# Side work of a hybrid attention and retention block issued in pairs between the dense matmuls

## The chip, the cores and the metric

One core of a Trainium2 chip. The time is the device time of one execution in microseconds; lower is better. The engines work in parallel and meet by semaphores: TensorE (PE; its weight loads are PEld), VectorE (DVE), ScalarE (ACT), GpSimd (POOL) and SyncE (SP), whose queue issues nearly all loads.

## The reference

One layer over 512 tokens of width 1024, in float32:

```python
h = rms_norm(x, norm_gain)
sb_q, sb_k, sb_v, sb_g, r_q, r_k, r_v, r_g, m_sb, m_ret = split(h @ w_in)
# attention, 8 heads of 128: w[t,s] = sigmoid(z) * prod over s<j<t of (1 - sigmoid(z_j)), s < t
out_a = stick_breaking(rms_norm(q), rms_norm(k), v) * silu(sb_g)
# retention, 4 heads of 256: (q.k) * gamma^|t-s| over the same chunk of 64 and all earlier ones
out_b = rms_norm(retention(rotary(r_q), rotary(r_k) / 16, r_v)) * silu(r_g)
merged = sigmoid(m_sb + b0) * (out_a @ w_branch_sb) + sigmoid(m_ret + b1) * (out_b @ w_branch_ret)
y = x + merged @ w_out
```

## The kernel before

Every float32 operand is split in a high and a low half (`split`: ScalarE copies the high half, VectorE subtracts for the low one), and each product is three matmuls (`mm3`): high x high, high x low, low x high.

**Dense groups.** `dense` makes one 512 x 512 output over 8 blocks of k and 4 banks j: 96 matmuls of 512 columns, twelve for each k. Their order: qk0, v0, sg0, qk1, qk2, v1, sg1, qk3, ma0, rqk0, pa0, ma1, pa1, rg0, then the value projection of the retention in products of quarters (rv), rqk1, rqk2, rg1, rqk3, mb0, mb1, pb0, pb1, fin0, fin1. PSUM has 5 banks for them and 3 (`side_psum`) for the side work.

**Side work.** Everything small on TensorE is written as generators, and `Interleaver` runs them between the dense matmuls: `dense` calls `work.step()` (L249) after every six of them (after j = 1 and j = 3, not after the last of the group), so a group has 15 steps. A generator that yields n is resumed n steps later. There is one queue, first in, first out (only `token_sums` is put at its head): the next generator starts when the one ahead of it has ended, in the same step. `matmul`, `transpose` and `load` are kept in program order (`tc.keep_in_program_order`), so the order of these calls is the order on TensorE and on SP; the other engines' order is planned by the framework.

**What the generators do.** `post` of `qk_group` waits 8 steps (W_QK) and transposes the normed q and k, four transposes for each of 4 blocks of tokens, with ScalarE and VectorE making their halves. `attention` works on two heads of 4 blocks each, 8 blocks; in round n it issues the scores of block n (L577 on: three matmuls, VectorE's mask, two sigmoids on ScalarE, a scan and a product on VectorE), the values of a head whose fourth block was weighted in the round before (twelve matmuls, the gate, a split), and the weights of block n - 2 (b + 1 transposes, a split into `wT_pair`), each followed by a yield of 1 (W_Z, W_W). Scores of block b are at least 256 and up to 512 columns wide. `retention` issues four score pieces (`rz`, 2 steps apart, W_RZ), two value pieces (`ro`) and two pieces of four transposes (`rt`).

**Where it must be done.** `work.drain(ready)` resumes the head of the queue until a condition holds, without regard to what it yields and without dense matmuls between. `pa0` multiplies the attention's outputs: its act for block k is `branch_act(oa)`, which drains until head k's output `oa[k]` is made. `ret(0)` (its dense group is rqk0) drains until `oa[5]` is there, rotates q and k on VectorE (`rope_group`) and adds the generator of retention head 0.

Of the kernel before, what the change touches and what calls it, by code (L numbers as in the profile page):

```python
# [15 lines left out]
NT = S // P  # L16
# [22 lines left out]
W_QK, W_Z, W_W = 8, 1, 1  # L39
W_RQ, W_RZ, W_RO, W_RN = 8, 2, 2, 5  # L40
# [32 lines left out]
def hybrid_block(ctx, tc, x, x_t, vecs, w_in, w_rv, w_a, w_b, w_o, cos_t, sin_t, decay, out):  # L73
# [13 lines left out]
    def f32(ap):  # L87
        return ap.bitcast(F32)
# [4 lines left out]
    def transpose(*a):  # L93
        tc.keep_in_program_order(nc.tensor.transpose(*a))

    def mm3(ps, a, b, first, last):

        matmul(ps, a[0], b[0], start=first, stop=False)
        matmul(ps, a[0], b[1], start=False, stop=False)
        matmul(ps, a[1], b[0], start=False, stop=last)  # L100

    def side_psum(name):
        return ps_a.tile([P, S], F32, tag="a", name=name)

    def T_tile(name, dtype=F32R):
        return big.tile([P, 4, S], dtype, tag="T", bufs=4, name=name)
# [14 lines left out]
    def bk_tile(name, dtype=F32):  # L121
        return tmp.tile([P, 2, S], dtype, tag="bk", bufs=3, name=name)
# [3 lines left out]
    def tmp_tile(name):  # L126
        return tmp.tile([P, S], F32, tag="tmp", name=name)
# [74 lines left out]
    def rsqrt(dst, ssq, n, width):  # L202
        t = small.tile([P, 16], F32, tag="ms", name="ms")
        nc.vector.tensor_scalar(t[:, :width], ssq, 1.0 / n, EPS, op0=ALU.mult, op1=ALU.add)  # L204
        nc.gpsimd.tensor_tensor(dst, t[:, :width], m_half[:, :width], op=ALU.pow)  # L205
# [49 lines left out]
    def proj(name, blocks, rows):  # L255
        return dense(name, lambda k: (xT_hi[:, k, :], xT_lo[:, k, :]), w_in, blocks, rows)
# [44 lines left out]
    def qk_group(p):  # L301

        ps = proj(f"qk{p}", ((C_Q + 256 * p, 256), (C_K + 256 * p, 256)), True)
        ss = small.tile([P, NT, 4], F32, tag="ss", name=f"ss{p}")
        raws = []
        for tb in range(NT):
            raw = tmp.tile([P, 4, P], F32, tag="qraw", bufs=4, name=f"qraw{p}_{tb}")
            nc.scalar.copy(raw, ps[tb].rearrange("p (h d) -> p h d", h=4))
            raws.append(raw)
        for tb in range(NT):  # L310
            sq = tmp_tile("sqq").rearrange("p (h d) -> p h d", h=4)
            nc.scalar.activation(sq, raws[tb], AF.Square)
            nc.vector.reduce_sum(ss[:, tb, :], sq, axis=mybir.AxisListType.X)
        rr = small.tile([P, NT, 4], F32, tag="rr", name=f"rr{p}")
        nc.vector.tensor_mul(ss, ss, rx2.rearrange("p (b o) -> p b o", o=1).broadcast_to([P, NT, 4]))
        rsqrt(rr.rearrange("p b h -> p (b h)"), ss.rearrange("p b h -> p (b h)"), HD, 16)
        nc.gpsimd.tensor_mul(rr, rr, rx.rearrange("p (b o) -> p b o", o=1).broadcast_to([P, NT, 4]))
        for tb in range(NT):
            nc.gpsimd.tensor_tensor(
                raws[tb], raws[tb],  # L320
                rr[:, tb, :].rearrange("p (h o) -> p h o", o=1).broadcast_to([P, 4, P]), op=ALU.mult,
            )

        def post():
            hi, lo = T_tile(f"qk_hi{p}"), T_tile(f"qk_lo{p}")
            yield W_QK
            for tb in range(NT):
                pt = side_psum(f"pqk{p}_{tb}").rearrange("p (h d) -> p h d", h=4)
                for j in range(4):
                    transpose(pt[:, j, :], raws[tb][:, j, :], ident)  # L330
                ts = slice(tb * P, (tb + 1) * P)
                for c, a in ((V_QG, 0), (V_KG, 2)):
                    g = vec[:, c : c + 1]
                    nc.scalar.activation(hi[:, a : a + 2, ts], pt[:, a : a + 2, :], AF.Copy, scale=g)
                    nc.vector.scalar_tensor_tensor(
                        lo[:, a : a + 2, ts], pt[:, a : a + 2, :], g, f32(hi[:, a : a + 2, ts]),
                        op0=ALU.mult, op1=ALU.subtract,
                    )
                yield 1
            qk_parts[p] = (hi, lo)  # L340

        work.add(post())
        if p == 0:
            work.add(token_norm_rows())
# [207 lines left out]
    def attention(heads, ready, v, gates):  # L552

        blocks = [(h, b) for h in heads for b in range(NT)]
        beta = {}

        def scores(h, b):
            hi, lo = qk_parts[h // 2]
            a, n = h % 2, (b + 1) * P
            ts = slice(b * P, n)  # L560
            z = side_psum(f"z{h}_{b}")
            m = max(n, 256)
            mm3(z[:, :m], (hi[:, a, ts], lo[:, a, ts]), (hi[:, 2 + a, :m], lo[:, 2 + a, :m]), True, True)
            nc.vector.tensor_add(z[:, ts], z[:, ts], neg_mask)  # L564
            bk = bk_tile(f"beta{h}_{b}")
            bt, keep = bk[:, 0, :], bk[:, 1, :]
            nc.scalar.activation(keep[:, :n], z[:, :n], AF.Sigmoid, scale=-sc)  # L567
            nc.scalar.activation(bt[:, :n], z[:, :n], AF.Sigmoid, scale=sc)
            nc.vector.tensor_tensor_scan(  # L569
                keep[:, :n][:, ::-1], keep[:, :n][:, ::-1], zero.broadcast_to([P, n]), 1.0,  # L570
                op0=ALU.mult, op1=ALU.add,
            )
            nc.vector.tensor_mul(bt[:, : n - 1], bt[:, : n - 1], keep[:, 1:n])
            beta[h, b] = bt

        def weights(h, b):
            hi, lo = wT_pair  # L577
            bt = beta.pop((h, b))
            pw = side_psum(f"pw{h}_{b}").rearrange("p (i t) -> p i t", t=P)
            for i in range(b + 1):  # L580
                transpose(pw[:, i, :], bt[:, i * P : (i + 1) * P], ident)
            ts = slice(b * P, (b + 1) * P)
            split(hi[:, : b + 1, ts], lo[:, : b + 1, ts], pw[:, : b + 1, :])

        def values(h):
            hi, lo = wT_pair
            po = side_psum(f"po{h}")
            cs = slice((h % 4) * P, (h % 4 + 1) * P)
            vv = v()
            for i in range(NT):  # L590
                t0 = min(i, NT - 2) * P
                mm3(po[:, t0:], (vv[i][0][:, cs], vv[i][1][:, cs]), (hi[:, i, t0:], lo[:, i, t0:]),
                    i == 0, i == NT - 1)
            o = tmp_tile(f"oa{h}")
            nc.vector.tensor_mul(o, po, gates()[h % 4])
            oa[h] = O_pair(f"oa{h}")
            split(oa[h][0], oa[h][1], o)

        for n in range(len(blocks) + 3):
            if n < len(blocks):  # L600
                scores(*blocks[n])
                yield W_Z
            if n >= 3 and blocks[n - 3][1] == NT - 1:
                while not ready():
                    yield 1
                values(blocks[n - 3][0])
                yield W_Z
            if 2 <= n < len(blocks) + 2:
                weights(*blocks[n - 2])
                yield W_W  # L610

    def rope_group(h, ready):

# [22 lines left out]
    def retention(h, qk, v, gates, made):  # L636
# [7 lines left out]
        for i in range(NT):  # L644
            n = S - i * P
            z = side_psum(f"rz{h}_{i}")
            ks = slice(i * P, (i + 1) * P)
            t0 = min(i, NT - 2) * P
            for d in range(2):
                mm3(z[:, t0:], (hi[:, 2 + d, ks], lo[:, 2 + d, ks]), (hi[:, d, t0:], lo[:, d, t0:]),  # L650
                    d == 0, d == 1)
            pf = tmp_tile(f"pf{h}_{i}")
            nc.vector.tensor_mul(pf[:, :n], z[:, i * P :], dec[:, :n])
            split(pT[0][:, i, i * P :], pT[1][:, i, i * P :], pf[:, :n])
            yield W_RZ
        yield 1
        c0 = (h % 2) * 256
        ss = small.tile([P, NT], F32, tag="rss", name=f"rss{h}")
# [29 lines left out]
        for e in range(2):  # L688
            pt = side_psum(f"rt{h}_{e}")
            for b in range(NT):  # L690
                transpose(pt[:, b * P : (b + 1) * P], raws[b // 2][:, b % 2, e * P : (e + 1) * P], ident)
            o = tmp_tile(f"ob{h}_{e}")
            c = V_RG + 2 * h + e
            nc.vector.scalar_tensor_tensor(
                o, pt, vec[:, c : c + 1], gates()[2 * (h % 2) + e], op0=ALU.mult, op1=ALU.mult
            )
            ob[2 * h + e] = O_pair(f"ob{h}_{e}")
            split(ob[2 * h + e][0], ob[2 * h + e][1], o)
            yield 1

    def branch_act(parts):
        def act(k):
# [68 lines left out]
    for g in range(2):  # L771
        ps = dense(f"fin{g}", lambda k: tuple(t[:, k % 4, :] for t in mt[k // 4]), w_o, ((S * g, S),), True)
        queue = nc.scalar if g == 0 else nc.sync
        for tb in range(NT):
            n = S // 2 if g == 1 and tb == NT - 1 else S
# [75 lines left out]
```

## Time and profile before

| | us |
|---|---|
| median of 3 runs | 658.37 (658.17 to 658.61) |
| profiled execution | 658.81 |
| its span, first to last instruction | 657.0 |
| PE busy | 650.5 |
| DVE busy | 393.7 |
| ACT busy | 276.2 |
| POOL busy | 65.6 |
| DMA, share of 16 engines, q1 | 31.4% |

A matmul's length in the profile is from its issue to its modelled end, and matmuls overlap: one of 512 columns is shown with 0.39 us and the next one starts 0.227 us after it. How long a piece of TensorE's stream takes is therefore read from the chain that ended last, which merges pieces in order of time and lists each with its share of the time and its number of matmuls. The page's line of the granted clock has full speed in all 40 slices.

### The profile page before, as it was taken

How to read it: one execution, taken by the hardware profiler on the slowest of the kernel's cores; microseconds unless marked ns; L12 is line 12 of the kernel's file. 1: busy time of each engine (PE TensorE's matmuls, PEld its weight loads, DVE VectorE, ACT ScalarE, POOL GpSimd, SP SyncE). 2: the span in 40 equal slices, each digit the busy share in tenths (PEclk: the TensorE clock that was granted, in tenths of full speed). 3: DMA queues.
4: the chain of work that ended last, by engine and by line, in shares of the span. 5: the costliest groups of instructions: out<-in, count | busy, mean ns of one | idle time of the engine just before them, and what ended most of it. 6: DMA issues, size and time to landing. Idle time of an engine off the chain costs nothing.

```text
span 657.0 us, 7987 instructions
## 1 busy us (share of the span) xinstructions
PE 650.5 (99%) x3073; PEld 539.7 (82%) x3073; DVE 393.7 (60%) x582; ACT 276.2 (42%) x439; POOL 65.6 (10%) x58
## 2 busy tenths in 40 slices
PE   9999999999999999999999999999999999999997
PEld 6788888888888888888888878888888888888885
DVE  6356863596497477664464876386673862554632
ACT  5744534564364564332733554333342442422310
POOL 0051001250000400000330100200100101000000
PEclk9999999999999999999999999999999999999999
DMA  8543223322322312332538522232322322225441
GB/s 280 202 128 96 65 64 97 97 64 66 97 64 65 97 64 65 103 95 89 210 97 299 126 55 65 81 96 65 108 69 81 97 64 82 81 97 165 156 157 64
DMA packets 42503, 69.22 MB, mean 105 GB/s; under 512 B 2913, under 2 KB 19553, under 8 KB 42209
## 3 DMA queue, kind: packets, MB, share of 16 engines
q1 hardware_dynamic: 41168, 65.55, 31.4%
q0 software_dynamic: 576, 2.10, 1.7%
q10 hardware_dynamic: 720, 1.07, 0.4%
q8 instruction: 24, 0.39, 0.3%
q14 instruction: 15, 0.11, 0.1%
HBM read 65.55 MB, written 2.10 MB: 103 GB/s over the span
## 4 chain that ended last, share of the span: by engine, by line
PE 94%; DMA 3%; DVE 1%; ACT 1%; SPq 0%; issue 0%; DVEq 0%; ACTq 0%
PE rqk_ps L91 13%; PE qk_ps L91 10%; PE v_ps L91 7%; PE sg_ps L91 7%; PE pa_ps L91 7%; PE mb_ps L91 7%; PE ma_ps L91 7%; PE rg_ps L91 7%; PE fin_ps L91 7%; PE pb_ps L91 7%; PE rv_y L91 3%; PE rv_p L91 2%; PE po L91 2%; PE z L91 2%; PE rz L91 2%; PE ro L91 2%
## 5 line engine op out<-in xcount | busy, mean ns | idle before, releaser
L91 PE MATMUL rqk_ps<-xT_hi,rqk_hi 128*128 128x512 f32 x128 | 50.9, 397 | 0.0
L91 PE MATMUL qk_ps<-qk_hi,xT_hi 128*128 128x512 f32 x128 | 50.5, 402 | 0.0
L91 PE MATMUL rqk_ps<-xT_hi,rqk_lo 128*128 128x512 f32 x128 | 50.0, 391 | 0.0
L91 PE MATMUL rqk_ps<-xT_lo,rqk_hi 128*128 128x512 f32 x128 | 50.0, 391 | 0.0
L91 PE MATMUL qk_ps<-qk_hi,xT_lo 128*128 128x512 f32 x128 | 49.2, 392 | 0.2 <-DVE xT_lo L176 0.2
L91 PE MATMUL qk_ps<-qk_lo,xT_hi 128*128 128x512 f32 x128 | 49.0, 390 | 0.0
L91 PE MATMUL pa_ps<-oa,pa_hi 128*128 128x512 f32 x128 | 39.6, 390 | 0.0
L91 PE MATMUL pb_ps<-ob,pb_hi 128*128 128x512 f32 x128 | 39.4, 389 | 0.0
L569 DVE TENSOR_TENSOR_SCAN beta<-beta,zero 128x128 f32<-128x128 f32 (+3 forms) x32 | 26.9, 840 | 7.5 <-ACT beta L567 7.5
L91 PEld LDWEIGHTS qk_ps<-qk_hi,xT_lo 128*128 128x128 f32 x128 | 23.9, 188 | 5.8 <-DVE xT_lo L176 0.6
L91 PEld LDWEIGHTS rqk_ps<-xT_hi,rqk_lo 128*128 128x128 f32 x128 | 24.0, 188 | 5.2
L91 PEld LDWEIGHTS pa_ps<-oa,pa_hi 128*128 128x128 f32 x128 | 23.9, 188 | 5.3 <-ACT rk L620 0.4
L91 PEld LDWEIGHTS qk_ps<-qk_hi,xT_hi 128*128 128x128 f32 x128 | 24.0, 188 | 5.2 <-ACT xT_hi L175 0.8
L91 PEld LDWEIGHTS pb_ps<-ob,pb_hi 128*128 128x128 f32 x128 | 24.0, 188 | 5.0
L91 PEld LDWEIGHTS rqk_ps<-xT_hi,rqk_hi 128*128 128x128 f32 x128 | 24.1, 188 | 4.4
L91 PEld LDWEIGHTS rqk_ps<-xT_lo,rqk_hi 128*128 128x128 f32 x128 | 24.1, 188 | 4.2
L91 PEld LDWEIGHTS qk_ps<-qk_lo,xT_hi 128*128 128x128 f32 x128 | 24.1, 188 | 4.1
L205 POOL TENSOR_TENSOR rr<-ms,m_half 128x16 f32<-128x16 f32 x4 | 11.7, 2913 | 150.7 <-DVE ms L204 150.7
L91 PE MATMUL v_ps<-v_hi,xT_hi 128*128 128x512 f32 x64 | 26.1, 408 | 0.0
L131 DVE TENSOR_TENSOR qk_lo<-qk_raw,qk_hi 128x1024 fp32r<-128x1024 f32 x14 | 17.1, 1223 | 14.9 <-ACT qk_hi L130 14.9
L567 ACT ACTIVATE beta<-z 128x128 f32<-128x128 f32 (+3 forms) x32 | 14.0, 436 | 28.5 <-DVE z L564 28.2
L91 PE MATMUL sg_ps<-xT_hi,sg_hi 128*128 128x512 f32 x64 | 25.8, 404 | 0.0
(255 smaller groups left out, 1738.4 us busy)
## 6 DMA issues: line engine op xcount, KB each, us to landing
rqk_raw<-in_w_in SPq DMA_DIRECT2D x32, 256.0 KB, 3.0
qk_raw<-in_w_in SPq DMA_DIRECT2D x28, 256.0 KB, 3.0
v_raw<-in_w_in SPq DMA_DIRECT2D x8, 512.0 KB, 3.8
sg_raw<-in_w_in SPq DMA_DIRECT2D x8, 512.0 KB, 3.6
ma_raw<-in_w_in SPq DMA_DIRECT2D x8, 512.0 KB, 3.6
pa_raw<-in_w_a SPq DMA_DIRECT2D x8, 512.0 KB, 4.0
rg_raw<-in_w_in SPq DMA_DIRECT2D x8, 512.0 KB, 3.7
mb_raw<-in_w_in SPq DMA_DIRECT2D x8, 512.0 KB, 3.6
```

The lines of the kernel that those rows point to most:

```text
L91: tc.keep_in_program_order(nc.tensor.matmul(*a, **k))
L131: nc.vector.tensor_sub(lo, src, f32(hi))
L205: nc.gpsimd.tensor_tensor(dst, t[:, :width], m_half[:, :width], op=ALU.pow)
L567: nc.scalar.activation(keep[:, :n], z[:, :n], AF.Sigmoid, scale=-sc)
L569: nc.vector.tensor_tensor_scan(keep[:, :n][:, ::-1], keep[:, :n][:, ::-1], zero.broadcast_to([P, n]), 1.0, op0=ALU.mult, op1=ALU.add,)
```

## The change

In `attention` the yield between scores and weights goes: a round issues the scores of block n and behind them, in the same step, the weights of block n - 2, and every round then yields 2 (W_Z + W_W). In a round with values, scores and weights stay apart, by a yield ahead of the values and one behind them. The transposes of q and k go out in two pieces of eight with 2 steps behind each, the retention's scores in pairs with 4 steps behind each pair, its last transposes together with 2 steps behind them.

```diff
@@ qk_group, post
-                yield 1
+                if tb % 2:
+                    yield 2
@@ attention
         for n in range(len(blocks) + 3):
             if n < len(blocks):
                 scores(*blocks[n])
+            if n >= 3 and blocks[n - 3][1] == NT - 1:
                 yield W_Z
-            if n >= 3 and blocks[n - 3][1] == NT - 1:
                 while not ready():
                     yield 1
                 values(blocks[n - 3][0])
                 yield W_Z
             if 2 <= n < len(blocks) + 2:
                 weights(*blocks[n - 2])
-                yield W_W
+            yield W_Z + W_W
@@ retention
             split(pT[0][:, i, i * P :], pT[1][:, i, i * P :], pf[:, :n])
-            yield W_RZ
+            if i % 2:
+                yield 2 * W_RZ
@@
             split(ob[2 * h + e][0], ob[2 * h + e][1], o)
-            yield 1
+        yield 2
```

## Rows read from the trace of the kernel before

**Rows 1.** The page, part 1 (busy us, share, instructions) and part 4 (chain).

```profile
PE 650.5 (99%) x3073; PEld 539.7 (82%) x3073; DVE 393.7 (60%) x582; ACT 276.2 (42%) x439; POOL 65.6 (10%) x58
...
PE 94%; DMA 3%; DVE 1%; ACT 1%; SPq 0%; issue 0%; DVEq 0%; ACTq 0%
```

**Rows 2.** The waits of TensorE: total us, times, longest us; first and last of four.

```profile
PE pi L91 <- DVE idle L184: 1.2, 1, 1.2
...
PE qk_ps L91 <- DVE xT_lo L176: 0.2, 1, 0.2
```

**Rows 3.** The chain that ended last, 160 to 176 us: start us, us, what.

```profile
162.65 12.26 PE sg_ps L91 x54
```

**Rows 4.** The chain, 64.5 to 82.5 us: attention of heads 0 and 1.

```profile
65.14 0.68 PE z L91 x3
65.83 1.37 PE sg_ps L91 x6
67.20 0.22 PE pw L94 x2
67.42 1.39 PE sg_ps L91 x6
68.81 0.35 PE z L91 x3
69.16 1.39 PE sg_ps L91 x6
...
80.51 1.93 PE po L91 x12
```

**Rows 5.** The chain, 268 to 292 us: the values of head 7 and pa0.

```profile
270.93 2.04 PE po L91 x12
272.97 1.37 PE rqk_ps L91 x6
274.34 16.62 PE pa_ps L91 x72
```

**Rows 6.** The timeline, 256 to 293 us: start us, us, engine, line, operation.

```profile
260.90 0.69 DVE L595 TENSOR_TENSOR oa<-po,sg 128x512 f32<-128x512 f32 x1 [0.26 <-PE po L91]
...
262.27 0.69 DVE L131 TENSOR_TENSOR oa<-oa,oa 128x512 fp32r<-128x512 f32 x1 [0.69 <-ACT oa L130]
...
263.56 0.39 PE L91 MATMUL z<-qk_hi 128*128 128x512 f32 x1
...
264.44 0.30 DVE L564 TENSOR_TENSOR z<-z,neg_mask 128x128 f32<-128x128 f32 x1 [1.27 <-PE z L91]
...
266.80 0.69 DVE L573 TENSOR_TENSOR beta<-beta 128x511 f32<-128x511 f32 x1
...
268.94 0.60 PE L94 MATMUL pw<-ident,beta 128*128 128x128 f32 x4
...
269.63 0.59 ACT L130 CAST wT<-pw 128x512 fp32r<-128x512 f32 x1 [1.35 <-PE pw L94]
...
270.25 0.69 DVE L131 TENSOR_TENSOR wT<-pw,wT 128x512 fp32r<-128x512 f32 x1 [0.82 <-ACT wT L130]
```

**Rows 7.** Busy us of each engine in two stretches: PE, PEld, DVE, ACT, POOL, clock, DMA.

```profile
230.00:273.00 43.00, 43.00 (x221) 35.95 (x220) 30.02 (x52) 21.26 (x43) 0.27 (x1) 1.00 0.25 80
273.00:288.30 15.30, 15.30 (x67) 12.31 (x66) 14.58 (x21) 6.93 (x10) 0.00 (x0) 1.00 0.24 70
```

**Rows 8.** The timeline, 190 to 198 us: first score matmul and last product.

```profile
190.31 0.40 PE L91 MATMUL z<-qk_hi 128*128 128x512 f32 x1
...
197.09 0.68 DVE L573 TENSOR_TENSOR beta<-beta 128x511 f32<-128x511 f32 x1
```

**Rows 9.** Stretches at the end (clock is third from last); TensorE's timeline at the start.

```profile
652.40:656.80 4.40, 0.42 (x2) 0.00 (x0) 0.76 (x2) 0.00 (x0) 0.00 (x0) 1.00 0.34 121
656.90:657.00 0.10, 0.00 (x0) 0.00 (x0) 0.00 (x0) 0.00 (x0) 0.00 (x0) 0.50 0.00 0
...
1.20 3.92 PE L91 MATMUL pi<-idle 128*128 128x512 bf16 x9 [1.20 <-DVE idle L184]
```

## What the change will do, predicted before it was run

> **What bounds the kernel now.** I read the page's busy shares first, then the chain that ended last, then the waits of TensorE, and only then single stages. TensorE is busy for 99% of the span and makes up 94% of the chain [rows 1]. The whole list of what it waited for is four lines, 2.4 us together, of which the first and the last stand here [rows 2]. So no other engine and no transfer sets the end: the time is the sum of the matmuls' issue times, and a change can gain only by cheaper matmuls in that stream, and lose by any wait that enters it.
>
> What does a matmul cost there? Undisturbed, 54 dense matmuls take 12.26 us, 0.227 us each, so six of them, which is one step of the interleaver, take 1.36 us [rows 3]. Next to side work the reader is to look at the six dense matmuls that follow each piece of it: after three score matmuls or after transposes they take 1.39 instead of 1.36 us, after the wide scores (four blocks) 1.37 us [rows 4]. A switch from side work back to dense work thus costs 0.01 to 0.03 us. That is all that grouping can save at one place. The granted clock is 1.00 through the stream.
>
> **Part 1: fewer switches.** In the attention, rounds n = 2, 3, 4, 5 and 7 of a pair of heads now put weights straight behind scores (in round 6 the values still come between): 5 switches fewer for each of 4 pairs, 20. The transposes of q and k go two at a time: 2 fewer for each of 4 groups, 8. The retention's scores: 2 fewer for each of 4 heads, 8; its last transposes: 1 fewer for each, 4. Sum 40 switches. At 0.03 us that is 1.2 us, at 0.01 us 0.4 us; I take 1.1, since most of them stand behind short matmuls. The matmuls themselves, the copies and the DMAs are the same in number.
>
> **Part 2: a longer way from the weights to the values.** Now the values follow the last weights by one step, and the matmul that needs the low half of the weights waits: 12 value matmuls take 2.04 us there [rows 5] and 1.93 us elsewhere [rows 4]. After the change three steps lie between. It happens four times, once for each pair; three of the four go (the fourth is part 3): 0.3 us gained.
>
> **Part 3: the steps.** This is the part that decides. A dense group gives 15 steps. Before, a pair of heads issues 8 scores, 8 weights and 2 values, one in each step: 17 steps from first to last, and the next generator starts one step after. After, every round yields 2, also the rounds that hold only scores (n = 0, 1) or only weights (n = 8, 9), and a round with values yields one more ahead of them and one behind. First scores to last values is 10 rounds x 2, 2 more in round 6 and 1 in round 10: 23 steps, and the next generator starts 3 steps later. A pair costs 6 + 2 = 8 steps more; the generators of the transposes cost 12 as before.
>
> For heads 0 and 1 this is free: their queue was empty for 8 steps. From then on the generators follow each other without a gap, so heads 2 and 3 end 6 steps late, heads 4 and 5 14, heads 6 and 7 22. Before, the values of head 7 go out 6 matmuls ahead of pa0 [rows 5]. pa0 needs them only in its last k (`branch_act` drains until they are there), that is 6 + 84 matmuls, or 14 steps and a bit, later. 22 steps late against 14 to spare is 8 short. At the drain in pa0, scores of (7, 3), weights of (7, 1), (7, 2), (7, 3) and the values of head 7 are still to come, and they go out one behind the other, with no dense matmul between them. TensorE keeps its order, so everything behind waits too.
>
> **What that drain costs.** It is a chain through all engines, and each link has its row from a time when head 7's block stood alone. Scores from first matmul to the end of the product with the suffix: 263.56 to 267.49, 3.93 us (mask, two sigmoids, scan, product) [rows 6]. Four transposes, copy to the high half, subtraction for the low half: 268.94 to 270.94, 2.0 us, with 0.1 for the hand over ahead of it 2.1 us [rows 6]. The second value matmul can start then; from there to the end of the last is 2.0 us of the 2.04 of [rows 5]. Product with the gate, high half, low half: 260.90 to 262.96, 2.06 us [rows 6]; then the second matmul of pa0's k = 7 can start. With 0.1 us for the other hand overs: 10.2 us. TensorE has work in it for scores 0.68, transposes of 2, 3 and 4 blocks at 0.11 a block 0.22 + 0.33 + 0.44, values 1.93 and one dense matmul 0.23: 3.8 us [rows 3, 4]. Idle: 6.4 us. Nothing that I can name hides it: what could (dense matmuls) stands behind it in the same queue.
>
> **Queueing on VectorE and ScalarE.** Two things make links longer. In the drain, the copies of weights (7, 1) and (7, 2) stand among the sigmoids; and pa0 now holds attention of heads 6 and 7 beside the rotation of `rope_group`, which before had the stage to itself and filled VectorE for 14.58 of 15.30 us [rows 7]. A stretch with two heads of attention has VectorE busy for 30.02 of 43.00 us, some 16 of it, by my estimate from the lengths of its rows, attention, the rest casts of weights and of q and k [rows 7]. About one and a half heads, 12 us, join the 14.6 us, in a stage of some 27 us of matmuls (15 steps, the scores, transposes and values of it): nearly full. The bounds for one link: from below 3.93 us as above; from above the scores that fell beside a group's eviction, 190.31 to 197.77, 7.46 us [rows 8], 3.5 us more. Of a round in the stage: weights now follow their scores by 4 steps, 5.5 us and some 1.2 us of side work, and reuse the bank of the round just before (2 steps, some 3.5 us) where three steps lay between; a chain of 7.46 us would make TensorE wait 0.8 us, the usual one of under 4 us not. So 0 to 3.5 us in the drain and 0 to 2.5 us in the rounds; I take 1.0 in all, near the lower end, because in the whole of before, with its group evictions beside the attention, TensorE's list of waits has no scores and no weights at all [rows 2].
>
> **DMAs.** The retention's decay for head 0 is loaded 16 steps later (163 instead of 147 of the interleaver's count) on SP's queue, behind it the second half of ma1's weights. It waits for the buffer that the transposes of weights (7, 1) free, at the head of the drain; the weights behind it are needed some 8 us after that drain ends. I cost it at nothing, with that stretch and the drain as its cover; without it, one load.
>
> **Sum.** The profiled execution took 658.81 us with a span of 657.0, the median of the runs is 658.37; the sum goes on the span and is carried over to the median. Switches -1.1, values -0.3, drain +6.4, queueing +1.0: +6.0. Span 663.0, median 664.4.
>
> **Rivals.**
> - The VectorE becomes the bound of pa0: rotation and attention queue behind each other, the drain's first link is 7.46 us and rounds wait 0.8 us each: +3.5 and up to +2 more than I take, 666 to 670. For it: the 14.58 of 15.30 us. Against it: the rotation's products have pauses while ScalarE makes high halves, and in the stretches of attention alone TensorE never waited for scores [rows 2].
> - The clock falls. In this trace it stands at 1.00 in the stretch of 4.4 us of which matmuls fill the first 0.42, and at 0.50 behind it, at the span's end [rows 9]; the level of 0.50 is 1.2 GHz of the two, 1.2 and 2.4. In the drain TensorE has one gap of 2.7 us (scores to the last transposes) and four under 1.7 us, with short work between. If it fell, nine matmuls at the start, when the engine came from rest, took 3.92 us, 0.43 us each, against 0.227 [rows 3, 9]; about as many at that pace cost 1.8 us: 666.2. The Trainium skill, "TensorE: Matmul & The Clock Gate", section "A second HAM failure mode: psum-queue depth-cycling", says that many short idles between groups of matmuls make the clock swing between its levels. It speaks against this change; no stretch of this trace has such idles, so no row bears it out.
> - Not slower: the drain doesn't happen. It takes 8 steps: if the values of head 7 went out by step 160 instead of 168, only parts 1 and 2 are left, 658.4 - 1.4 = 657.0. It decides at the 8 steps; against it is the count, which for the kernel before gives just the places seen in the trace (head 7's values six matmuls ahead of pa0).
> - The change groups but the switch cost isn't saved, because two pieces together disturb the dense work as much as two alone: 665.5, inside the range.
>
> **How the numbers follow.** Forecast with little queueing 0.63 (its own range 662.5 to 666), VectorE as the bound 0.20, clock 0.10, not slower 0.05, another loss 0.02. The range reaches from 661.5 (drain at 6.4 less 0.7, larger gains) to 669.5. A measurement of this kernel tells about 0.2% (1.3 us) from no change. Faster by over that 0.03, within it 0.03, slower 0.94.
>
> **What would show it.** The waits of TensorE and of its weight loads after should list pw, po and pa_ps, some 6 us, all in one stretch ahead of pa0's last twelve matmuls, about 290 us into the span. Dense matmuls after side work: 1.39 us for six as before, in about 40 places fewer. The values of heads 1, 3 and 5 should take 1.93 us. Wrong would be: no stretch near the end of pa0 without dense matmuls; waits of z or pw in the rounds of several us (the first rival); a granted clock under 1.00 there.

## The result and the profile after

| | before | after |
|---|---|---|
| median, us | 658.45 (658.17 to 658.61) | 673.9 (673.08 to 674.74) |
| ratio | | 1.0237 [1.0225, 1.025] |
| profiled execution, us | 658.81 | 673.88 |
| its span, us | 657.0 | 672.1 |
| PE busy, us | 650.5 | 655.2 |
| mean granted clock | 1.000 | 0.991 |

Slower, as forecast, but by 15.4 us where 6.0 were expected, and above the stated range, which ended at 669.5 us. The page after, its parts 1 and 4, against [rows 1]:

```profile
PE 655.2 (97%) x3073; PEld 544.6 (81%) x3073; DVE 396.5 (59%) x582; ACT 274.4 (41%) x439; POOL 66.2 (10%) x58
...
PE 94%; DVE 3%; ACT 1%; issue 1%; DMA 0%; SPq 0%; DVEq 0%; ACTq 0%
```

Two things are to be seen. The instructions are the same in number on every engine, yet TensorE is busy 4.7 us longer: some matmuls were slower. And VectorE and ScalarE, 1% each of the chain before, now hold 4% of it together. Part of that is waiting of TensorE; not all of it is, since the chain runs through VectorE and ScalarE from 262.4 us on, while TensorE still had dense matmuls up to 270.8.

The waits of TensorE (engine, tile and line waiting, what ended the wait; total us, times, longest us). Of [rows 2] the first is still there; new are, above all, these:

```profile
PE pa_ps L91 <- ACT oa L130: 3.1, 2, 1.7
PE z L91 <- ACT beta L569: 3.1, 1, 3.1
PE pw L94 <- DVE beta L574: 2.8, 1, 2.8
...
PE po L91 <- ACT wT L130: 0.7, 1, 0.7
...
PE pa_ps L91 <- DVE oa L131: 0.5, 2, 0.2
```

`pw`, `po` and half of `pa_ps` are the drain that was forecast. The wait of `z`, and the other half of `pa_ps`, were not in the sum.

The chain that ended last, 255 to 314 us (start us, us, what); the lines shown lie in `pa0`:

```profile
273.65 0.28 ACT beta L569
...
273.98 1.59 PE z L91 x3
...
289.53 1.22 DVE ma_lo L131
290.75 0.61 DVE oa L596
...
291.38 0.63 ACT oa L130
...
292.03 0.70 DVE oa L131
...
292.78 1.42 PE pa_ps L91 x5
...
297.55 1.24 DVE beta L570
...
298.88 0.70 DVE beta L574
...
299.72 0.64 PE pw L94 x4
...
301.80 3.32 PE po L91 x11
...
305.14 0.70 DVE oa L596
...
306.52 0.70 DVE oa L131
...
307.27 4.32 PE pa_ps L91 x11
```

Read it in three pieces. From 295.5 on stands the drain: scores of (7, 3), the last weights, the values of head 7, the gate and the halves, one behind the other, then `pa0`'s k = 7 (not every link is shown). Ahead of it, at 290 to 292.8, is the same walk through gate and halves for head 6, ahead of k = 6. And at 274 scores, which never waited before, wait for a sigmoid of other scores. Note also the values: 3.32 us for eleven, where twelve took 1.93 [rows 4].

The granted clock says why. Stretches of `pa0` and what follows (us, busy time of PE, PEld, DVE, ACT, POOL, then the clock, the DMA share and GB/s):

```profile
262.00:272.00 10.00, 8.91 (x42) 7.14 (x40) 9.96 (x16) 5.19 (x8) 0.00 (x0) 1.00 0.17 53
274.10:277.40 3.30, 3.30 (x9) 2.48 (x10) 3.28 (x9) 2.23 (x5) 0.00 (x0) 0.50 0.21 81
290.00:301.30 11.30, 5.86 (x29) 4.15 (x28) 5.69 (x10) 3.20 (x7) 0.00 (x0) 1.00 0.33 105
301.40:304.70 3.30, 3.12 (x11) 2.71 (x11) 0.34 (x1) 0.00 (x0) 0.00 (x0) 0.50 0.07 25
304.90:308.10 3.20, 1.53 (x7) 0.88 (x7) 1.44 (x3) 0.62 (x1) 0.00 (x0) 1.00 0.00 0
308.30:311.60 3.30, 3.30 (x9) 2.52 (x8) 1.82 (x3) 0.41 (x1) 0.00 (x0) 0.50 0.00 0
```

Three stretches at 0.50, 1.2 GHz; between them 1.00. Each stands behind idles of TensorE: 3.1 us ahead of the scores at 273.98; 2.8 and 0.7 us in the drain, ahead of its last transposes and of the values; and 1.4 and 0.2 us ahead of the first matmuls of k = 7 (1.53 of 3.20 us busy in that row). And the first row of the list has VectorE at 9.96 of 10.00 us.

Last the timeline around the two waits that were missed, and the start of the drain (start us, us, engine, line, operation, idle before it and what ended that):

```profile
262.11 0.68 DVE L626 TENSOR_TENSOR rm<-rqk_ps,sr 128x512 f32<-128x512 f32 x1
...
264.49 0.28 PE L91 MATMUL z<-qk_hi,qk_lo 128*128 128x256 f32 x1
...
270.53 0.39 PE L91 MATMUL pa_ps<-oa,pa_lo 128*128 128x512 f32 x1
...
271.73 0.69 DVE L630 TENSOR_TENSOR rm<-rm,rm 128x512 f32<-128x512 f32 x1
...
272.94 0.29 DVE L565 TENSOR_TENSOR z<-z,neg_mask 128x128 f32<-128x128 f32 x1
...
273.98 0.73 PE L91 MATMUL z<-qk_hi 128*128 128x512 f32 x1 [3.06 <-ACT beta L569]
274.51 0.63 PE L91 MATMUL z<-qk_lo,qk_hi 128*128 128x512 f32 x1
274.93 0.63 PE L91 MATMUL z<-qk_hi,qk_lo 128*128 128x512 f32 x1
...
290.07 0.28 PE L91 MATMUL po<-wT,v_lo 128*128 128x256 f32 x1
292.05 0.50 PE L91 MATMUL pa_ps<-oa,pa_hi 128*128 128x512 f32 x1 [1.70 <-ACT oa L130]
292.78 0.50 PE L91 MATMUL pa_ps<-oa,pa_hi 128*128 128x512 f32 x1 [0.23 <-DVE oa L131]
...
295.53 0.40 PE L91 MATMUL z<-qk_hi 128*128 128x512 f32 x1
```

The mask at 272.94 is that of block (6, 1). Its scores were ready at 264.77, 8.17 us earlier, but on VectorE it stands behind the rotation of retention head 0 (`rm`, from 261.33 to 272.4 with the casts of `pa0`'s weights between). Only after the mask and two sigmoids is its PSUM bank free, at 273.93, which is 9.16 us after the last score matmul; and the scores of (6, 3) need that bank, since the other two of the three side banks went to the scores of (6, 2) and the transposes of (6, 0).

**The account of the span.** Before to after, in the profiled executions: +15.1 us. The grouping itself -1.2 (the span of `e1_paced`, below; by the medians it is 0.5). The drain: from the first score matmul of (7, 3) to the second matmul of k = 7, 295.53 to 307.27, is 11.74 us, and at full clock, in `e7_first_and_fill`, 10.37; less 3.8 us of TensorE's own work that is 6.6. Head 6's output: its last value matmul starts at 290.07, so that the next could go at 290.19 (256 columns, 0.12 us from start to start), but k = 6 starts at 292.05, and its next matmul comes 0.50 us late: 2.4. The scores of (6, 3): the dense matmul ahead of them starts at 270.53, so they could go at 270.76; they went at 273.98: 3.2. Sum 11.0. What is left, 4.1 us, has no wait, and is known to some 0.7 us only, as the grouping's share shows. I put it down to the clock. Priced by rows, its falls come to 4.6 us: half of the 3.4 us that the first stretch lasts, 1.7; 11.74 less 10.37 in the drain, 1.4; and at k = 7 the eleven matmuls from 307.27 on, which take 4.32 us and at full clock 2.83, 1.5. `e6_fill` tests it.

### The profile page after: what moved, and what is told of

Read it like the earlier page. It is cut to its first block, busy times and chain, and to the rows that moved or that the text cites. A ratio compares the mean times of both kernels' runs of the same rounds, so it can differ in the third digit from the quotient of the medians.

```text
span 672.1 us, 7988 instructions
## 1 busy us (share of the span) xinstructions
PE 655.2 (97%) x3073; PEld 544.6 (81%) x3073; DVE 396.5 (59%) x582; ACT 274.4 (41%) x439; POOL 66.2 (10%) x58
## 4 chain that ended last, share of the span: by engine, by line
PE 94%; DVE 3%; ACT 1%; issue 1%; DMA 0%; SPq 0%; DVEq 0%; ACTq 0%
PE qk_ps L91 13%; PE rqk_ps L91 13%; PE ma_ps L91 7%; PE mb_ps L91 7%; PE rg_ps L91 6%; PE fin_ps L91 6%; PE pb_ps L91 6%; PE sg_ps L91 6%; PE v_ps L91 6%; PE pa_ps L91 6%; PE rv_y L91 3%; PE rv_p L91 2%; PE rz L91 2%; PE z L91 2%; PE po L91 2%; PE ro L91 2%
## 5 line engine op out<-in xcount | busy, mean ns | idle before, releaser
L91 PE MATMUL pa_ps<-oa,pa_hi 128*128 128x512 f32 x128 | 42.4, 411 | 3.6 <-ACT oa L130 3.1
L131 DVE TENSOR_TENSOR rqk_lo<-rqk_raw,rqk_hi 128x1024 fp32r<-128x1024 f32 x16 | 19.6, 1224 | 22.3 <-ACT rqk_hi L130 22.2
L130 ACT CAST wT<-pw 128x128 fp32r<-128x128 f32 (+3 forms) x32 | 13.7, 427 | 36.8 <-PE pw L94 36.8
L130 ACT CAST rqk_hi<-rqk_raw 128x1024 fp32r<-128x1024 f32 x16 | 16.8, 1052 | 24.4 <-PE rqk_ps L91 18.1
```

The source lines that it names most:

```text
L91: tc.keep_in_program_order(nc.tensor.matmul(*a, **k))
L130: nc.scalar.copy(hi, src)
L131: nc.vector.tensor_sub(lo, src, f32(hi))
```

## The experiments

The first question was whether the pairs or the lateness cost the time; the next, what each wait costs by itself. Diffs are against the changed kernel unless said otherwise. Ratios are to the kernel before on the same chip.

### e1_paced: pairs, but as many steps as before

```diff
         for n in range(len(blocks) + 3):
+            due = n >= 3 and blocks[n - 3][1] == NT - 1
+            pair = 2 <= n < len(blocks) and not due
             if n < len(blocks):
                 scores(*blocks[n])
-            if n >= 3 and blocks[n - 3][1] == NT - 1:
-                yield W_Z
+                if not pair:
+                    yield W_Z
+            if due:
...
                 weights(*blocks[n - 2])
-            yield W_Z + W_W
+                yield W_W + W_Z * pair
```

> All grouping of the change is kept, but the attention takes no more steps than before: a step of 2 only where scores and weights go out together, 1 after a single piece. Theory A (lateness: the loss comes from the 8 extra steps of each pair of heads, which push heads 6 and 7 into pa0): no drain in pa0, no wait of the scores there, 657.0 us, that is the 1.1 to 1.4 us of saved switches and value waits below the kernel before. Rival B (grouping itself costs, since banks and products of a round have less room): TensorE waits in the rounds, 662 to 674 us.

Measured: 657.71 us, ratio 0.9993 [0.9984, 1.0002]; span 655.8, clock 1.00. Its whole list of TensorE's waits:

```profile
PE pi L91 <- DVE idle L184: 1.2, 1, 1.2
PE rv_y L91 <- DVE rv_c L510: 0.7, 2, 0.4
PE qk_ps L91 <- ACT xT_hi L175: 0.3, 1, 0.3
```

No `z`, no `pw`, no `po`, no `pa_ps`. Grouping costs nothing. What it brings is 1.2 us by the spans of the two profiled executions and 0.5 by the medians, which the interval doesn't tell from nothing.

### e2_apart_late: scores and weights apart again, as many steps as after

```diff
                 scores(*blocks[n])
+                if pair:
+                    yield W_Z
...
                 weights(*blocks[n - 2])
-            yield W_Z + W_W
+            yield W_W + W_Z * (not pair)
```

> Scores and weights go out one step apart, as before the change, but every round takes as many steps as in the changed kernel; the transposes and the retention stay grouped. Theory A: as slow as the changed kernel plus some 20 switches at 0.03 us, 674.5 us (672 to 677), with the same drain ahead of pa0's last twelve matmuls. Rival B: the rounds have their room again, 658 to 660 us.

Measured: 674.37 us, ratio 1.0245 [1.0231, 1.0259]. The waits are those of after to a tenth (`z` 3.1, `pw` 2.8, `pa_ps` 3.1), and the same three stretches are at half clock. With the attention's pairs undone, all of the loss stays: it is the steps.

### e3_rest_alone: the attention as before, only transposes and retention grouped

```diff
             if n < len(blocks):
                 scores(*blocks[n])
-            if n >= 3 and blocks[n - 3][1] == NT - 1:
                 yield W_Z
+            if n >= 3 and blocks[n - 3][1] == NT - 1:
...
                 weights(*blocks[n - 2])
-            yield W_Z + W_W
+                yield W_W
```

> The attention as before the change; only the transposes and the retention's scores are grouped (20 switches fewer). Theory A: 0.2 to 0.6 us below the kernel before, 657.9 us. Rival B: at or above 658.4 us, because eight transposes in a row wait for banks.

Measured: 657.79 us, ratio 0.9992 [0.9983, 1.0001]. This part of the change does no harm, and its gain too is below what can be told.

### e4_eleven_late: late, but within the 14 steps

Rounds with only weights, and rounds with values, yield 1 at their end, so that head 7 is 11 steps late and not 22.

```diff
-            yield W_Z + W_W
+            due = n >= 3 and blocks[n - 3][1] == NT - 1
+            if n < len(blocks) and not due:
+                yield W_Z + W_W
+            else:
+                yield W_W
```

> The changed kernel, with rounds of only scores at 2 steps but rounds of only weights and rounds with values at 1 behind them: a pair costs 4 steps more in place of 8, and the values of head 7 go out 11 steps late of 14 to spare, in step 157, so nothing is drained. It parts the two losses of theory A: if only the drain costs, 657 to 658 us; if the rotation beside the attention costs by itself (scores waiting behind it on VectorE, as the 8.2 us before the mask of block (6, 1) in the changed kernel), 660 to 664 us, with a wait of TensorE for scores or weights of head 6 or 7 within 15 us of the start of pa0.

Measured: 664.29 us, ratio 1.0091 [1.0077, 1.0105], just above the 660 to 664 us expected. The drain is gone, as the 14 steps say, and 6 us of loss are still there. The wait, and the clock behind it:

```profile
PE po L91 <- ACT beta L569: 4.3, 1, 4.3
```

```profile
264.00:272.00 8.00, 8.00 (x40) 6.78 (x40) 8.00 (x15) 3.83 (x6) 0.00 (x0) 1.00 0.23 70
...
276.50:279.70 3.20, 2.46 (x6) 1.76 (x7) 2.58 (x6) 1.27 (x4) 0.00 (x0) 0.50 0.00 0
```

Now it is the values of head 6 that need a bank, held by scores still without a mask, 4.3 us, and 6.8 us at half clock go with it (276.41 to 283.24; the first part is shown). VectorE is busy for 8.00 of 8.00 us ahead of it. There is thus a loss without any drain, and `e8_eleven_late_first` and `e9_no_rotation` ask whether the rotation beside the attention makes it.

### e5_scores_first: the scores' work ahead of the rotation on VectorE

```diff
-            nc.vector.tensor_add(z[:, ts], z[:, ts], neg_mask)
...
-            nc.vector.tensor_mul(bt[:, : n - 1], bt[:, : n - 1], keep[:, 1:n])
+            with tc.high_priority():
+                nc.vector.tensor_add(z[:, ts], z[:, ts], neg_mask)
...
+                nc.vector.tensor_mul(bt[:, : n - 1], bt[:, : n - 1], keep[:, 1:n])
```

> The changed kernel, with the mask, sigmoids, scan and product of the scores planned ahead of other work; on VectorE the masks of blocks (6, 1) to (7, 0), which stood behind the rotation's last operations, then stand among them, TensorE's order is untouched. Theory A: TensorE's wait of 3.1 us for the scores (6, 3) goes, and with it the stretch at half clock behind it (8 matmuls at 0.43 in place of 0.23 us, 1.6 us); the drain stays: 669.1 us. Rival (the wait is for something that VectorE's order doesn't reach): 673 to 674 us.

The block under `high_priority` holds the mask, both sigmoids, the scan and the product. Measured: 670.52 us, ratio 1.019 [1.0174, 1.0205]. The wait of `z` is gone, but another one has come, and VectorE is no emptier:

```profile
PE pw L94 <- ACT beta L570: 2.3, 1, 2.3
```

```profile
264.00:276.00 12.00, 12.00 (x59) 10.00 (x57) 11.96 (x21) 7.18 (x14) 0.00 (x0) 1.00 0.20 55
278.50:281.90 3.40, 3.35 (x17) 2.85 (x18) 3.29 (x9) 2.08 (x3) 0.00 (x0) 1.00 0.00 0
```

So the order on VectorE was the cause of the wait of `z`, but only of part of its cost: VectorE has no time left there, and now the transposes of (6, 2) wait until a sigmoid of another block is done. The gain was 3.4 us of the 4.8 expected. The clock stays at 1.00 behind this wait (second row), and in the whole of this execution it falls once, in the drain.

### e6_fill: dummy matmuls in the five waits

```diff
+    def fill(name, n):
+        t = ps_mm.tile([P, S], F32, tag="mm", name=name)
+        for j in range(n):
+            matmul(t, xT_hi[:, 0, :P], xT_hi[:, 0, :], start=True, stop=True)
...
+            if (h, b) == (6, 3):
+                fill("fill_z", 12)
...
+            if (h, b) == (7, 3):
+                fill("fill_pw", 10)
...
+            if h == 7:
+                fill("fill_po", 2)
...
+                fill(f"fill_oa{k}", 6 if k == 6 else 5)
```

> The changed kernel with 35 dense matmuls more, whose result nobody reads, at the five places where TensorE waits (12 ahead of scores (6, 3), 6 and 5 ahead of pa0's k = 6 and 7, 10 ahead of weights (7, 3), 2 ahead of the values of head 7), each group shorter than the wait that it stands in. Theory: the waits stay as long and only the clock's falls go: three stretches at half clock cost some 4.6 us, so 669.3 us with the clock at 1.00. Rival (the clock costs nothing that the waits don't cover): 673.9 us; if the added matmuls come out at their own price, 682 us.

Measured: 670.4 us, ratio 1.0185 [1.0168, 1.0202]. The stretches that stood at 0.50:

```profile
273.00:277.40 4.40, 3.70 (x17) 2.50 (x16) 4.38 (x11) 2.53 (x7) 0.00 (x0) 1.00 0.42 119
...
301.40:304.70 3.30, 3.07 (x17) 2.48 (x16) 0.95 (x2) 0.26 (x1) 0.00 (x0) 1.00 0.03 12
304.90:311.60 6.70, 6.26 (x26) 4.94 (x27) 4.68 (x6) 1.22 (x2) 0.00 (x0) 1.00 0.00 0
```

TensorE does 35 matmuls more, and the kernel is 3.5 us faster: the dummies stand where it waited, and the clock no longer falls. That prices the clock at 3.5 us at least, where 4.6 were expected; the 4.1 of the account are 0.6 more, and one wait is new here, ahead of the transposes of (6, 1):

```profile
PE pw L94 <- DVE wT L136: 0.4, 1, 0.4
```

### e7_first_and_fill: both, with 23 dummy matmuls (none ahead of the scores of (6, 3))

On top of `e5_scores_first`, the dummies of `e6_fill` but for these:

```diff
-            if (h, b) == (6, 3):
-                fill("fill_z", 12)
```

> Both: scores planned first, and the 23 added matmuls of the drain and of pa0's k = 6 (none ahead of scores (6, 3)). Theory: only the drain's chain and the wait for head 6's output are left, at full clock: 669.1 - 3.0 = 666.1 us, that is 658.4 - 1.3 + 6.4 + 2.4. Rival (the two losses overlap): above 668 us.

Measured: 669.7 us, ratio 1.0178 [1.0163, 1.0193], 3.6 us above what was expected. The wait of 2.3 us of `e5_scores_first` is still there, ahead of the weights of (6, 2), and in the profiled execution 3.4 us at half clock behind it:

```profile
277.50:280.60 3.10, 3.10 (x10) 2.51 (x10) 2.57 (x7) 1.20 (x3) 0.00 (x0) 0.50 0.00 0
```

Its four executions differ in this: with a mean clock of 0.999 two took 669.13 and 669.16 us, with 0.996 the other two took 670.24 and 671.01. One fall of 3.4 us at half clock lowers the mean of such a span by 0.003; so, by the mean clock, the same idle was followed by a fall in two executions and by none in two, and the fall cost 1.1 to 1.9 us. What this kernel is worth is the drain at full clock. It starts, in the timeline, and goes on, in the chain:

```profile
294.83 0.39 PE L91 MATMUL z<-qk_hi 128*128 128x512 f32 x1
```

```profile
301.09 1.97 PE po L91 x11
...
305.20 2.83 PE pa_ps L91 x11
```

From 294.83 to 305.20 it is 10.37 us.

### e8_eleven_late_first: the yields of e4_eleven_late and the order of e5_scores_first

The split of the weights is put ahead on VectorE as well.

```diff
-            split(hi[:, : b + 1, ts], lo[:, : b + 1, ts], pw[:, : b + 1, :])
+            with tc.high_priority():
+                split(hi[:, : b + 1, ts], lo[:, : b + 1, ts], pw[:, : b + 1, :])
```

> The kernel in which head 7's values go out 11 steps late, within the 14 to spare, with the scores' and the weights' work on VectorE and ScalarE planned first. Theory A (late steps cost nothing as long as the slack lasts and VectorE's order doesn't hold the banks back): the wait of 4.3 us for the values goes, 657.3 to 658.5 us. Rival (VectorE is too full there whatever the order): 660 us and more.

Measured: 657.17 us, ratio 0.9986 [0.9977, 0.9995]; span 656.2, clock 1.00. No wait for a bank is left in its list, and one of 0.2 us for the weights. VectorE has some room, 7.74 of 8.00 us:

```profile
264.00:272.00 8.00, 8.00 (x41) 6.78 (x40) 7.74 (x15) 4.80 (x11) 0.00 (x0) 1.00 0.29 87
```

Against `e4_eleven_late` only the planned order of VectorE's and ScalarE's work differs, and 7.1 us are back. With half the lateness VectorE keeps up, so here the order decides. Late by 11 steps, the kernel loses nothing. It beats the kernel before, though by little, 0.05 to 0.23%, and the changed kernel by 16.7 us.

### e9_no_rotation and e10_no_rotation_fill: without the rotation

For retention head 0 the kernel leaves out the rotation, twelve operations of VectorE: its q and k are split as they come.

```diff
+        if h == 0:
+            for j in range(4):
+                split(hi[:, j, :], lo[:, j, :], ps[j])
+            return hi, lo
```

> The changed kernel without the rotation of retention head 0: its q and k are split as they come (12 products and sums of VectorE, some 7 us, left out). Theory (the rotation's load on VectorE, not its order alone, makes the waits of the scores and weights in the rounds of pa0): no wait of TensorE for scores or weights in pa0 ahead of the values of head 6, the half clock behind it gone too: 673.9 - 3.2 - 1.6 = 669.1 us, below the kernel with the scores planned first (670.5). Rival (the rounds of 2 steps are too short for the banks by themselves): a wait of over 1 us stays, 670 us or more.

Measured: 670.01 us, ratio 1.0181 [1.0165, 1.0197], 0.9 us above what was expected; the four executions run from 668.88 us at a mean clock of 0.995 to 671.62 at 0.989. The scores wait for nothing any more, and VectorE has 8.02 of 10.00 us where it had 9.96; the two later stretches at half clock stay, of which the first is shown:

```profile
262.00:272.00 10.00, 10.00 (x48) 8.31 (x47) 8.02 (x14) 6.49 (x13) 0.00 (x0) 1.00 0.19 58
296.60:300.00 3.40, 3.37 (x10) 2.74 (x11) 0.69 (x1) 0.00 (x0) 0.00 (x0) 0.50 0.15 58
```

The rotation beside the attention costs some 3.9 us with the clock that it takes along. With the 23 dummy matmuls of `e7_first_and_fill`, in the drain and ahead of k = 6, as well:

```diff
+            if (h, b) == (7, 3):
+                fill("fill_pw", 10)
...
+            if h == 7:
+                fill("fill_po", 2)
...
+                fill(f"fill_oa{k}", 6 if k == 6 else 5)
```

> The same without the rotation of head 0, and with the 23 added matmuls in the drain and ahead of pa0's k = 6 that keep the clock up. Only the drain (6.5 us by the trace of the changed kernel) and the wait for head 6's output (2.5 us) are left beside the gain of the grouping (1.2 us in the spans): 658.0 - 1.2 + 9.0 = 665.8 us, clock 1.00. Rival (a loss that I haven't named): 667 us or more.

Measured: 666.68 us, ratio 1.0127 [1.0113, 1.0141], 8.4 us above before and 0.9 above what was expected, 0.3 short of the rival's bound; clock 1.00 throughout. That leaves the drain, 6.6, and head 6's output, 2.4, less the 1.2 of the grouping: 7.8 us by the account. It closes within 0.6 us.

### e11_paced_first and e12_before_first: is there something in the order alone?

The order of `e8_eleven_late_first`, and nothing else, on `e1_paced` and on the kernel before.

```diff
+            with tc.high_priority():
+                nc.vector.tensor_add(z[:, ts], z[:, ts], neg_mask)
...
+            with tc.high_priority():
+                split(hi[:, : b + 1, ts], lo[:, : b + 1, ts], pw[:, : b + 1, :])
```

> All grouping with no more steps than before, and the scores' and weights' work planned first. Theory (nothing but switches and value waits are left to gain): 657.2 us, as the kernel that is 11 steps late with the work planned first. Rival (the order on VectorE gains by itself): below 656.5 us.

> The kernel before with only the scores' and weights' work planned first. Theory (TensorE never waited for them before): no difference, 658.0 us (within 0.5). Rival (the order and not the grouping made the kernel that is 11 steps late 0.9 us faster): 657.2 us.

Measured: 657.64 us, ratio 0.9989 [0.998, 0.9997], and 658.15 us, ratio 0.9998 [0.9989, 1.0007]. The order brings nothing where nothing waits. Which of `e1_paced`, `e8_eleven_late_first` and `e11_paced_first` is the best isn't settled by these runs: their intervals overlap.

## Why the prediction was wrong in size

**Right: the steps.** Head 7 comes 22 steps late against a slack of 14, the drain stands where it was put, and with 11 steps (`e4_eleven_late`) there is none. `e2_apart_late` shows that the steps, not the pairs, are the whole loss.

**Right: the drain's length.** 10.2 us were built from single rows of before, link by link; the chain at full clock took 10.37. Its first link took 4.05 us in the changed kernel (3.93 taken). Idle 6.6 against 6.4. The copies of other blocks among the links cost 0.1 us there: the long casts on VectorE fell elsewhere.

**Right within the measurement: parts 1 and 2.** -1.4 taken, -1.2 by the spans; the values of heads 1, 3 and 5 take 1.93 us now. The medians don't tell this gain from none. The load of the retention's decay, costed at nothing, shows up in no wait.

**Failed: the step that costed only head 7.** "pa0 needs them only in its last k" is true of head 7. But every k of `pa0` has its own head, and 14 steps of slack for head 7 are none for head 6 once it is late as well: its values went out in the last step of k = 5, and k = 6 waited for gate and halves, 2.4 us. The numbers for it were in [rows 6], 2.06 us; the question was not asked.

**Failed: queueing, taken at 1.0 us.** I bounded a round by the worst chain seen before, 7.46 us [rows 8], and so a wait by 0.8 us. In `pa0` a bank came free only 9.16 us after the last score matmul, and TensorE waited 3.2. The row came from a stage in which attention met a group's eviction, not the rotation; how much VectorE would have to do, some 26.6 us in 27, was about right (25.2 us from `pa0`'s first matmul, at 262.9, to the drain at 295.5), but it stood crowded at the start, 9.96 of 10.00 us, and the "nearly full" was priced near the lower end. The step that failed in it is the reading of order: [rows 2] showed that TensorE never waited in stages of attention alone, which says nothing of a stage where eleven operations of the rotation stand ahead of a mask in VectorE's order. The first rival, given 0.20, was this mechanism: its rounds waited, though in one place and not in each, while its drain was no longer.

**Failed: the clock, given 0.10 and 1.8 us and left out of the sum.** It fell three times, for 4.1 us by what the account leaves and 4.6 by rows. The price of one fall was about the 1.8 that I took (1.4 to 1.7 us in the account); that there would be three was not foreseen. It was priced from [rows 9] alone, where 0.50 stands behind the idle at the span's end and no work was left there to be slowed by it. The Trainium skill, "TensorE: Matmul & The Clock Gate", section "A second HAM failure mode: psum-queue depth-cycling", tells of a bf16 kernel in which frequent short idles between groups of matmuls make the clock swing between its two levels. The trace agrees as far as it goes, 0.50 three times and 1.00 between, each fall behind idles of 1.4 to 3.1 us. But the 1.7 us ahead of k = 6 were followed by no fall, and the 2.3 us ahead of the transposes of (6, 2) by none in `e5_scores_first` and by one in the profiled execution of `e7_first_and_fill`. So the length of an idle alone doesn't tell; what does, these runs don't show.

The forecast of the span was +6.0. With head 6 (+2.4), the rounds (3.2 for the 1.0 taken, +2.2) and the clock (+4.1) it is +14.7, against +15.1 in the span. That they agree is no test of the clock's 4.1, which was what the account left; `e6_fill`, with 3.5 us, is.

What stays open besides: why VectorE's planned order put eleven operations of the rotation ahead of the mask of (6, 1) but not of (6, 0). Only what moves it was tried.

## What to carry to other kernels

Where side work is paced by steps, count for each consumer, not just the last, how many steps of slack its producer has, and then ask what the later work meets on the engines that were off the path: a full VectorE stage that harmed nobody holds PSUM banks as soon as TensorE needs them back. And price an idle of TensorE in a dense stream at more than its length: here some 12 us of waits took about 4 us of clock with them.

## What the runs showed of the hardware

A fall of the clock cost 1.4 to 1.7 us here: in the stretches at half clock 512-column matmuls start 0.43 us apart (274.51 to 274.93) and not 0.227. The same kernel, `e7_first_and_fill`, has, by its mean clock, a fall behind one of its waits in two executions and none in two others. Work thrown into the waits, 35 matmuls whose products nobody reads, made the kernel 3.5 us faster, with the clock at 1.00 throughout, though waits of up to 0.5 us were left in those places. And where side work returns to dense matmuls the switch is nearly free in this kernel: 40 switches fewer moved the span by 1.2 us and the median by nothing that can be told.
